# A trace of matrix products: TensorE's last products in a loop of one turn, and one block of the last long piece moved from TensorE to VectorE

## The chip, the cores and the metric

The kernel runs on one core of one Trainium2 chip. The core has TensorE (matrix products, PE in the profile; its weight loads are PEld), VectorE (DVE), ScalarE (ACT), GpSimd (POOL) and SyncE (SP), and 16 DMA engines that bring data from the chip's memory. The metric is device time in microseconds (us) of one execution, from its start to its end; lower is better. A profiled execution also has a span: from its first to its last recorded instruction.

## The reference

For each of 8 pairs of 2176 x 2176 matrices in float32 the trace of the product is wanted:

```python
def setup_inputs():
    B, N = 8, 2176
    return {
        "a": np.random.randn(B, N, N).astype(np.float32),
        "b": np.random.randn(B, N, N).astype(np.float32),
    }

def reference(a, b):
    prod = np.matmul(a, b)
    traces = np.diagonal(prod, axis1=1, axis2=2).sum(axis=-1)
    return traces.astype(np.float32)
```

The trace of a product needs no product: it is the sum over all i and k of a[i, k] * b[k, i]. So each matrix is read once, one of the two is transposed, and the rest is an elementwise product with a sum. The two inputs hold 303 MB.

## The kernel before

**Layout.** 2176 is 17 x 128. A matrix is split into three groups of rows: two of 6 x 128 and one of 5 x 128. The tiles `a_six` and `five` hold rows of a in bfloat16 (the DMA converts on the way), `rows_b` holds rows of b (and shares its first five planes with `five`), and `at` holds the transposed a, cut to fit b's rows: 17 planes of 2176 columns each, in the same places as b's.

**The main loop, once for each of 8 batches.** GpSimd issues the loads of a and b (L182). TensorE transposes a in 128 x 128 blocks into three slots of PSUM (`aT`, L242 and L245), in a hardware loop of eight turns written as `nc.Fori` over TensorE alone (L226). `hint_back_edge=True` puts a prefetch hint at the head of the loop body; the loop ends with an addition to its register and a compare-and-branch. ScalarE (L276) and VectorE (L302) copy the slots to `at`. VectorE then multiplies `at` by b's rows and sums along the row (L291), one number for each partition into `sums`.

**The last batch.** Here b arrives in ten pieces (`pieces`), the later ones smaller, so that little work is left when the last byte is down. Planes 0 to 15 come in seven pieces (`whole`). The last plane, 16 (`END`), comes in three: columns 6*128 to 2176 (eleven blocks of 128, 352 KB in the list of DMA issues), columns 2*128 to 6*128 (four blocks, 128 KB) and columns 0 to 2*128 (two blocks, 64 KB). GpSimd issues all of them about 50 us ahead of the end; each counts on a semaphore of its own (`d_late`). Behind the issues GpSimd steps a semaphore that nobody reads 20 times (`unread`, L219).

The work on them is shared:

- VectorE does the first 13 blocks of each whole plane (`SHARE` columns) and of the eleven-block piece the first ones (`N - CLOSE * P` is where its part ends; with `CLOSE = 6` that is five blocks, 640 columns), in the loop `for k, piece in enumerate(pieces[:len(whole) + 1])`.
- TensorE does the rest as matrix products of `at` and `rows_b` blocks that add up in one PSUM tile, `trace_ps`: the wanted sum is on the diagonal of that tile. For the 16 whole planes this is a second hinted loop (L252 to L256), four blocks in a turn, each turn waiting for `landed`. For the three pieces of the last plane the products are written out one by one (L262): the last six blocks of the eleven-block piece, then four, then two, each group waiting for its own piece. The last product counts on `added`.

VectorE waits for `added`, multiplies `trace_ps` by the identity and sums it (also L291, `diagonal<-identity,trace_ps`). TensorE adds up the partitions of `sums` with a product by ones (L332), after a wait for all of VectorE's parts (`parts`). VectorE reduces that to eight numbers (L334), and SyncE stores them (L339). A barrier of all engines ends the program.

**Order.** Every engine runs its instructions in the order in which they are written here; waits are on semaphores. In the program TensorE's stream is: the big loop, one product that clears `trace_ps` (L250), the loop at L252, the twelve products of L262, the sum at L332, and the closing barrier.

Of the kernel before, what the change touches and what calls it, by code (L numbers as in the profile page):

```python
# [22 lines left out]
def kernel(  # L23
# [6 lines left out]
    nc = tc.nc  # L30
    P = 128
    BATCH, N, N2 = a.shape
    assert N == N2 and N % P == 0
    NT = N // P
# [6 lines left out]
    f32 = mybir.dt.float32  # L41
    MUL, ADD = mybir.AluOpType.mult, mybir.AluOpType.add
    SLOTS = 3
    ON_TENSOR, TAKEN, CLOSE = 4, 4, 6
    SHARE = N - ON_TENSOR * P

    const = ctx.enter_context(tc.tile_pool(name="const", bufs=1))
# [15 lines left out]
    trace_ps = psum.tile([P, P], f32, tag="trace")  # L63
# [47 lines left out]
    def flat(t):  # L111
        return t.rearrange("p r k -> p (r k)")
# [10 lines left out]
    class Piece:  # L123
# [9 lines left out]
    END = NT - 1  # L133
    pieces = [
        Piece(0, 5), Piece(5, 9), Piece(9, 11), Piece(11, 13), Piece(13, 14), Piece(14, 15),
        Piece(15, 16), Piece(END, NT, 6 * P, N), Piece(END, NT, 2 * P, 6 * P), Piece(END, NT, 0, 2 * P),
    ]
# [6 lines left out]
    with tc.tile_critical(no_gpsimd_drain=True):  # L144
        def counted(name):
            return Counted(nc, name)
# [4 lines left out]
        d_late = [counted(f"late{n}") for n in range(len(pieces))]  # L151
# [6 lines left out]
        product, added = counted("product"), counted("added")  # L158
# [64 lines left out]
        pe = nc.tensor  # L223
        pe.wait_ge(ready.sem, 3)
        alone = OrderedEngineSet([pe.engine])
        with nc.Fori(0, BATCH, engines=alone, hint_back_edge=True):  # L226
            for n, (moves, _, _) in enumerate(tiles):
                use, k = divmod(n, SLOTS)
# [22 lines left out]
        x, y = flat(at), flat(rows_b)  # L251
        with nc.Fori(SHARE, SHARE + END * N, N, engines=alone, hint_back_edge=True) as first:  # L252
            pe.wait_ge(landed, 1).then_inc(landed, -1)  # L253
            for c in range(ON_TENSOR):
                block = bass.ds(first + c * P, P)
                pe.matmul(trace_ps, x[:, block], y[:, block], start=False, stop=False)  # L256
        for k, piece in enumerate(pieces):
            if piece.v1 == NT:
                pe.wait_ge(d_late[k].sem, 16)
                for c in range(N - CLOSE * P if piece.hi == N else piece.lo, piece.hi, P):  # L260
                    block = slice(END * N + c, END * N + c + P)
                    ins = pe.matmul(  # L262
                        trace_ps, x[:, block], y[:, block],
                        start=False, stop=piece.lo == 0 and c + P == piece.hi,
                    )
        added.by(ins)


        act = nc.scalar
        for n in range(BATCH):  # L270
            for t in on_scalar:
# [4 lines left out]
                ins = act.copy(out=dst, in_=view(slots[t % SLOTS]))  # L276
# [19 lines left out]
        for n in range(BATCH):  # L296
            for t in on_vector:
# [4 lines left out]
                ins = dve.tensor_copy(out=dst, in_=view(slots[t % SLOTS]))  # L302
# [14 lines left out]
        for k, piece in enumerate(pieces[:len(whole) + 1]):  # L317
# [8 lines left out]
            x, y = (t[:, piece.v0:piece.v1, piece.lo:N - CLOSE * P if close else SHARE] for t in (at, rows_b))  # L326
# [50 lines left out]
```

## Time and profile before

| | us |
|---|---|
| median of three runs | 707.95 (707.53 to 708.2) |
| the profiled execution, its own time | 707.8 |
| span of that execution | 705.8 |
| busy in the span: PE / PEld | 207.5 / 184.1 |
| busy in the span: DVE / ACT / POOL | 382.5 / 205.9 / 25.5 |

The granted TensorE clock had a mean of 0.643 over the span and was 0.50 from 670 us to the end.

How to read the lines shown below. The page begins with the span; its row "DMA" gives the mean busy share of the 16 DMA engines in 40 equal slices of the span, in tenths (9 is 90% or more), and rows that begin with q give a DMA queue, its packets, megabytes and share of the 16 engines' time. The chain of waits is followed back from the last instruction; each row has the start in us, the length in us and what the time was spent on. A timeline row has the start, the length, the engine, the source line, the operation, the tiles written and read, their shapes and a count of merged instructions; in square brackets stand the idle time of the engine before it and what ended it. A row of DMA issues ends with the size and the time from issue to landing. A row by source line gives the shortest, median and longest duration in ns, then the first and the last start in us; PEldq and POOLq are the instructions of an engine's queue that are not counted as its work, such as branches, register moves and semaphore steps.

### The profile page before, as it was taken

The page shows a single profiled execution, that of the slowest core. Times are in us where ns is not written, and L with a number is a line of the kernel's source. Part 1 is how long each engine was busy: PE and PEld are TensorE (multiplying, and loading weights), DVE is VectorE, ACT ScalarE, POOL GpSimd, SP SyncE. Part 2 cuts the span into 40 slices and gives each one's busy share as a digit, 9 for nine tenths or more (in the row PEclk, how much of TensorE's full clock was granted, in tenths as well). Part 3 has the DMA queues.
Part 4 walks back from the last instruction along what each step waited for, and adds up shares of the span by engine and source line. Part 5 has one row for each costly group of instructions (what it writes and reads, how often), then busy time and mean ns, then how long its engine had stood idle before and what let it go on. Part 6 is the DMA issues. An engine that isn't in the chain of part 4 may idle for free.

```text
span 705.8 us, 3821 instructions
## 1 busy us (share of the span) xinstructions
PE 207.5 (29%) x1575; PEld 184.1 (26%) x1575; DVE 382.5 (54%) x101; ACT 205.9 (29%) x162; POOL 25.5 (4%) x47
## 2 busy tenths in 40 slices
PE   0335013440134401244013430124301353015633
PEld 0334012440124401243013430124301242014522
DVE  0105487153971539716396163961639617395388
ACT  1427003470034600336004450044500454005800
POOL 1000000000000000000000000000000000001100
PEclk9859555685556955569556785567855677555955
DMA  9999999999999999999999999999999999999998
GB/s 235 215 216 207 231 207 213 217 225 213 223 218 213 206 214 228 213 213 229 209 211 230 214 210 223 219 213 209 231 207 213 229 213 213 224 218 213 214 212 160
DMA packets 7846, 152.12 MB, mean 216 GB/s; under 512 B 674, under 2 KB 930, under 8 KB 1442
## 3 DMA queue, kind: packets, MB, share of 16 engines
q0 software_dynamic: 7696, 150.96, 99.8%
q10 hardware_dynamic: 144, 1.11, 0.5%
q8 instruction: 1, 0.02, 0.0%
q14 instruction: 3, 0.02, 0.0%
q1 hardware_dynamic: 2, 0.00, 0.0%
HBM read 303.04 MB, written 0.00 MB: 429 GB/s over the span
## 4 chain that ended last, share of the span: by engine, by line
DMA 34%; another core or an unknown queue 28%; DVE 15%; ACT 13%; PE 7%; issue 2%; POOL 1%; SPq 0%; DVEq 0%; POOLq 0%
DMA rows_b<-in_a_dram 21%; DVE at L291 15%; ACT at L276 13%; DMA rows_b<-in_b_dram 7%; DMA a_six<-in_a_dram 6%; PE aT L242 6%; PE aT L245 1%; POOL rows_b L182 1%; PE trace_ps L262 0%; DVE diagonal L291 0%; PE total L332 0%; DVE result L334 0%; DVE sums L291 0%; DVEq L308 0%
## 5 line engine op out<-in xcount | busy, mean ns | idle before, releaser
L276 ACT COPY at<-aT 128x1536 bf16<-128x1536 bf16 (+3 forms) x160 | 202.6, 1359 | 458.2 <-DVE sums L291 357.2
L291 DVE CUSTOM_DVE_ANT_0 at<-at,rows_b 128x10880 bf16<-128x10880 bf16 (+3 forms) x18 | 278.3, 15469 | 98.5 <-DMA rows_b<-in_b_dram 83.7
L302 DVE COPY at<-aT 128x1536 bf16<-128x1536 bf16 (+1 forms) x48 | 80.1, 1669 | 207.6 <-PE aT L242 156.1
L242 PE MATMUL aT<-identity,rows_b 128*128 128x128 f32 x240 | 55.4, 422 | 368.4 <-PEq L235 282.3
L242 PEld LDWEIGHTS aT<-identity,rows_b 128*128 128x128 f32 x240 | 47.1, 220 | 374.8 <-issue 283.2
L242 PE MATMUL aT<-identity,a_six 128*128 128x128 f32 x576 | 90.5, 320 | 93.7 <-SPq L173 80.5
L242 PEld LDWEIGHTS aT<-identity,a_six 128*128 128x128 f32 x576 | 83.3, 205 | 100.3 <-issue 89.4
L245 PE MATMUL aT<-identity,a_six 128*128 128x128 bf16 x480 | 34.3, 221 | 10.8 <-ACT at L276 9.5
L245 PEld LDWEIGHTS aT<-identity,a_six 128*128 128x128 bf16 x480 | 29.4, 119 | 15.2 <-ACT at L276 13.1
L291 DVE CUSTOM_DVE_ANT_1 at<-at,rows_b 128x3328 bf16<-128x3328 bf16 (+2 forms) x4 | 23.0, 5790 | 6.1 <-DMA rows_b<-in_b_dram 6.1
L182 POOL DMA_DIRECT2D rows_b<-in_b_dram x24 | 14.2, 613 | 330.0 <-PE aT L245 330.0
L245 PE MATMUL aT<-identity,rows_b 128*128 128x128 bf16 x200 | 17.7, 266 | 0.0
L245 PEld LDWEIGHTS aT<-identity,rows_b 128*128 128x128 bf16 x200 | 17.3, 135 | 0.5
L256 PE MATMUL trace_ps<-rows_b,at 128*128 x64 | 11.3, 285 | 20.6 <-PEq L253 20.6
L182 POOL DMA_DIRECT2D rows_b<-in_a_dram x8 | 4.6, 576 | 293.6 <-DVE sums L291 292.8
L256 PEld LDWEIGHTS trace_ps<-rows_b,at 128*128 x64 | 6.7, 104 | 25.2 <-issue 23.5
L182 POOL DMA_DIRECT2D a_six<-in_a_dram x9 | 6.1, 674 | 0.0
L284 DVE MEMSET ones<- 128x1 f32 x1 | 0.1, 59 | 8.1 <-ACT rows_b L142 8.1
L142 ACT CAST rows_b<-rows_b 128x2176 bf16<-128x2176 f32 x1 | 2.0, 2004 | 3.4 <-DMA rows_b<-in_a_dram 3.4
L262 PE MATMUL trace_ps<-rows_b,at 128*128 128x128 bf16 x12 | 1.5, 310 | 0.7 <-DMA rows_b<-in_b_dram 0.7
L142 ACT ACT_TABLE_LOAD x1 | 1.3, 1283 | 1.1 <-PEq L361 1.1
L291 DVE DVE_READ_ACCUMULATOR2_ANT sums<- 128x1 f32 x17 | 1.4, 83 | 0.0
(17 smaller groups left out, 4.3 us busy)
## 6 DMA issues: line engine op xcount, KB each, us to landing
a_six<-in_a_dram POOLq DMA_DIRECT2D x7, 6528.0 KB, 54.5
rows_b<-in_b_dram POOLq DMA_DIRECT2D x7, 6528.0 KB, 52.2
rows_b<-in_b_dram POOLq DMA_DIRECT2D x8, 2720.0 KB, 21.9
rows_b<-in_a_dram POOLq DMA_DIRECT2D x7, 2720.0 KB, 24.7
a_six<-in_a_dram POOLq DMA_DIRECT2D x2, 3264.0 KB, 47.0
rows_b<-in_a_dram POOLq DMA_DIRECT2D x1, 2176.0 KB, 14.8
rows_b<-in_b_dram POOLq DMA_DIRECT2D x1, 2176.0 KB, 31.0
rows_b<-in_b_dram POOLq DMA_DIRECT2D x2, 1088.0 KB, 38.0
```

The costliest lines, as they stand in the source:

```text
L142: nc.scalar.copy(out=five[:, 0, :], in_=words)
L182: count.by(gp.dma_start(out=dst, in_=src), 16)
L242: last = pe.transpose(ps[:, place, :], src, identity32)
L245: last = pe.transpose(ps16[:, place * P:(place + 1) * P], src, identity16)
L256: pe.matmul(trace_ps, x[:, block], y[:, block], start=False, stop=False)
L262: ins = pe.matmul(trace_ps, x[:, block], y[:, block], start=False, stop=piece.lo == 0 and c + P == piece.hi,)
L276: ins = act.copy(out=dst, in_=view(slots[t % SLOTS]))
L284: ready.by(dve.memset(ones, 1.0))
L291: return dve.tensor_tensor_reduce(out=x if out is None else out, in0=x, in1=y, scale=1.0, scalar=0.0, op0=MUL, op1=ADD, accum_out=acc,)
L302: ins = dve.tensor_copy(out=dst, in_=view(slots[t % SLOTS]))
```

## The change

The products of L262 are put into a hardware loop of one turn, on TensorE alone, with the same kind of hint as the two loops before it. Its count comes from a register that is set to 1 just ahead. `CLOSE` goes from 6 to 5: of the eleven-block piece TensorE now does the last five blocks (eleven products in all) and VectorE the first six (768 columns).

```diff
-    ON_TENSOR, TAKEN, CLOSE = 4, 4, 6
+    ON_TENSOR, TAKEN, CLOSE = 4, 4, 5
...
-        for k, piece in enumerate(pieces):
-            if piece.v1 == NT:
-                pe.wait_ge(d_late[k].sem, 16)
-                for c in range(N - CLOSE * P if piece.hi == N else piece.lo, piece.hi, P):
-                    block = slice(END * N + c, END * N + c + P)
-                    ins = pe.matmul(
-                        trace_ps, x[:, block], y[:, block],
-                        start=False, stop=piece.lo == 0 and c + P == piece.hi,
-                    )
-        added.by(ins)
+        once = nc.alloc_register(pe.engine, "once")
+        pe.reg_mov(once, 1)
+        with nc.Fori(0, pe.snap(once, min_val=1, max_val=BATCH), engines=alone, hint_back_edge=True):
+            for k, piece in enumerate(pieces):
+                if piece.v1 == NT:
+                    pe.wait_ge(d_late[k].sem, 16)
+                    for c in range(N - CLOSE * P if piece.hi == N else piece.lo, piece.hi, P):
+                        block = slice(END * N + c, END * N + c + P)
+                        ins = pe.matmul(
+                            trace_ps, x[:, block], y[:, block],
+                            start=False, stop=piece.lo == 0 and c + P == piece.hi,
+                        )
+            added.by(ins)
```

On TensorE's queue the built program gains, between the loop at L252 and the sum, three register moves and a prefetch hint ahead of the products, and an addition and a compare-and-branch behind them; a matrix product (with its weight load) is gone. The wait for each piece stays with that piece's first product. No other engine's instructions change but for VectorE's one longer product. Line numbers behind L256 are three higher after the change: L262 becomes L265, L332 becomes L335.

## The prediction

> **What bounds the kernel now.** I read the page first, then the chain of waits, then the timeline of the last microseconds, where all of the change lies.
>
> ```profile
> span 705.8 us, 3821 instructions
> ...
> DMA  9999999999999999999999999999999999999998
> ...
> q0 software_dynamic: 7696, 150.96, 99.8%
> ```
>
> The DMA engines are full in 39 of 40 slices, so up to the last byte no engine's work sets the time. What a change at the very end can move is the stretch behind that byte. The chain in order of time shows it:
>
> ```profile
> 650.02 3.64 POOL rows_b L182 x7
> 653.66 47.79 DMA rows_b<-in_b_dram
> 701.45 0.05 issue
> 701.50 1.48 PE trace_ps L262 x12
> 702.97 0.02 issue
> 703.00 0.29 DVE diagonal L291
> 703.28 0.02 DVE sums L291
> 703.30 0.04 issue
> 703.35 0.28 PE total L332 x2
> 703.63 0.02 issue
> 703.65 0.18 DVE result L334
> ```
>
> The transfer that starts at 653.66 lands at 701.45. TensorE's twelve written-out products (L262) follow, then VectorE's read of the diagonal, the sum on TensorE (L332) and VectorE's last reduction. The chain hides that inside the 1.48 us of L262 two more transfers land. The answers on the last DMA issues, and narrow stretches of the timeline, show them:
>
> ```profile
> 654.18 1.14 POOL L182 DMA_DIRECT2D rows_b<-in_b_dram  x2
> rows_b<-in_b_dram POOLq DMA_DIRECT2D x1, 128.0 KB, 47.9
> rows_b<-in_b_dram POOLq DMA_DIRECT2D x1, 64.0 KB, 47.7
> L262 PE MATMUL trace_ps<-rows_b,at x12: 289/314/314, 701.5 to 702.6; 128*128 128x128 bf16 x12
> 701.68 0.63 PE L262 MATMUL trace_ps<-rows_b,at 128*128 128x128 bf16 x4
> 702.13 0.61 PE L262 MATMUL trace_ps<-rows_b,at 128*128 128x128 bf16 x4
> 702.46 0.23 PEld L262 LDWEIGHTS trace_ps<-rows_b,at 128*128 128x128 bf16 x2
> ```
>
> The first row holds the last two issues. The four-block piece is issued at 654.18 and lands 47.9 later, at 702.08; the two-block piece is issued at about 654.70 and lands at 702.4. Four matmuls take 0.63 us and one 0.314, so one block follows another in (0.63 - 0.314) / 3 = 0.105 us. The first block of the four-block piece starts at 702.13, 0.05 us behind its landing, and the weights behind the last wait are loaded at 702.46, about 0.05 us behind theirs. The first piece started 0.05 us behind its landing too (701.45, 701.50). All three starts are set by landings.
>
> **One block from TensorE to VectorE.** The six blocks of the long piece, at 0.105 us each from 701.50, would let the next block start at 702.13, exactly where the landing lets it start. With five blocks TensorE is ready at 702.03 and waits for the same landing. So a whole block, 0.105 us, is removed and at most that is gained; I take nothing, because the start at 702.13 has the same 0.05 us behind its landing as the other two. From 702.13 the remaining six blocks run as before, to 702.97.
>
> VectorE's closing product grows from 640 to 768 columns:
>
> ```profile
> 699.74 1.89 DVE L291 CUSTOM_DVE_ANT_0 at<-at,rows_b 128x1664 bf16<-128x1664 bf16 x1 [0.15 <-DMA rows_b<-in_b_dram]
> ...
> 701.56 0.82 DVE L291 CUSTOM_DVE_ANT_0 at<-at,rows_b 128x640 bf16<-128x640 bf16 x1
> ...
> 703.00 0.29 DVE L291 CUSTOM_DVE_ANT_0 diagonal<-identity,trace_ps 128x128 bf16<-128x128 f32 x1 [0.61 <-PE trace_ps L262]
> ...
> 703.86 0.32 SPq L339 DMA_DIRECT2D out_dram<-result  x1
> ```
>
> 1,024 columns more cost 1.89 - 0.82 = 1.07 us, so 128 cost 0.13. VectorE had 0.61 us idle before the diagonal, which it needs at 703.00; 0.48 remain. Cost nothing; without that cover 0.13.
>
> **Entering the loop.** Between the old loop's exit and the first product TensorE's queue gets three register moves and a prefetch hint (and a branch that, like the one ahead of the loop at L252, should leave no row of its own). The same kinds, at L252:
>
> ```profile
> L252 PEldq MOVE  x2: 29/34/38, 668.6 to 668.8; - x2
> L252 PEldq BRANCH_PREFETCH_HINT  x1: 31/31/31, 668.7 to 668.7; - x1
> L252 PEldq ALU_OP  x1: 36/36/36, 700.5 to 700.5; - x1
> L252 PEldq COMPARE_BRANCH  x1: 80/80/80, 700.6 to 700.6; - x1
> ```
>
> Move, hint and move stand 0.1 us apart. The old loop's last branch ends at 700.6 + 0.08 = 700.7; four instructions at 0.1 bring TensorE to 701.1, and it waits for 701.45 anyway. Cover 0.35 us; cost nothing, and without the cover 0.4, of which the block taken away would give back 0.1.
>
> **Leaving the loop.** An addition and a compare-and-branch now stand between the last product and the sum L332 (L335 after). When can they run? The exit of the big loop at L226 tells:
>
> ```profile
> 666.55 0.53 PE L245 MATMUL aT<-identity,a_six 128*128 128x128 bf16 x6 [0.48 <-ACT at L276]
> L226 PEldq ALU_OP  x1: 36/36/36, 666.6 to 666.6; - x1
> L226 PEldq COMPARE_BRANCH  x1: 80/80/80, 666.7 to 666.7; - x1
> L249 PEldq EVENT_SEMAPHORE  x1: 51/51/51, 666.8 to 666.8; - x1
> ```
>
> Its addition runs as the last wait is released (666.55), before the six matmuls behind that wait end (667.08); the branch falls through in 0.08 us, and the next instruction is there 0.1 us on, although the loop was hinted to go back. In the new loop the last wait is released at 702.46, so the branch is done by about 702.7. The sum waits for VectorE until 703.30. Cover 0.6 us; cost nothing, provided that the code behind the loop is at hand.
>
> **The code behind the loop** is the open price. One 16 KB instruction transfer runs in the last microseconds of the trace, the only one on its queue:
>
> ```profile
> q0 software_dynamic: 222, 0.13, 90.7%
> q8 instruction: 1, 0.02, 6.1%
> ```
>
> That is the window from 701 to 702; a window from 701.6 to 701.8 has it starting there.
>
> ```profile
> q8 instruction: 1, 0.02, 30.6%
> ```
>
> 30.6% of 16 engines over 0.2 us is 0.98 us of one engine, so it is done at about 702.7. I take it for TensorE's: it starts about 1.1 us behind the exit of TensorE's loop, and no other engine leaves a loop. Then TensorE asks for code at or after 700.6 and has it 2.1 us later, with the twelve products already in its queue and covering the load. [...] If the missing code begins right behind the loop, the request falls at about 702.6 and the sum waits until 702.6 + 2.1 = 704.7 in place of 703.35: +1.4 us. The other bound is the slowest such load of the trace: GpSimd's run of 20 semaphore steps ends at 655.7, and a small instruction transfer follows only at 659.2.
>
> ```profile
> L219 POOLq EVENT_SEMAPHORE  x20: 17/17/17, 653.8 to 655.7; - x20
> q14 instruction: 1, 0.01, 20.1%
> ```
>
> The second row is the window 659.2 to 659.3. That is 3.5 us to the start under full DMA; with 0.98 for 16 KB it is 4.5, and the sum would come at 707.1, +3.8 us. At the other end the missing code is that of the closing barrier, which TensorE needs only at 704 and later: nothing. I take nothing for the forecast, because the added code is about six instructions and the boundary must fall in a narrow place to hurt; both ends stay in the range.
>
> [...]
>
> **Sum.** Block 0, VectorE 0, entry 0, exit 0, code 0: the profiled 707.8 us (a span of 705.8 and 2.0 around it) stays. It lies 0.15 below the median of 707.95; I forecast 708.0.
>
> **Rivals.**
> 1. Exposed code load. One mechanism: the code behind the one-turn loop is asked for only at 702.6, and the sum L335 stands behind it. For it: a code transfer does happen in the tail, and the change puts a stop in the queue between it and its cover. Against: the exit at L226 needed none. It gives 708 + 1.4 = 709.4, at most 711.8; it decides from the moment when the load takes more than 703.30 - 702.6 = 0.7 us.
> 2. Faster, because the code transfer leaves the last data microseconds. The packet starts at 701.77; the four-block piece lands at 702.08, so at most 0.3 us earlier, 707.6. Against: two of three pieces were down or almost down when it began. More than this no row offers.
> 3. The loop starts TensorE late: entry longer than its 0.35 us of cover. With twice the 0.4 counted, 0.45 late, less one block: +0.35, 708.3.
> 4. The change does not do what it says: the hint changes no code transfer, which stays at 701.8. Then 707.95.
>
> **How the numbers follow.** 0.2% of 708 is 1.4 us, about what a measurement of this kernel can tell from no change. Forecast with rival 4: 0.48, 707.6 to 708.3. Rival 1: 0.38, of which about 0.27 falls above 709.4, since its nearest row lies just at that bound and its far end well above. Rivals 2 and 3: 0.07 each; 0.05 of rival 2 stands for a gain beyond 1.4 us that I see in no row, and 0.03 of rival 3 for such a loss. So faster 0.05, slower 0.27 + 0.03 = 0.30, same 0.65. The range goes from 707.3 to 710.1: it leaves out the upper half of rival 1's far part and a larger gain.
>
> **What would show it.** Right: the first product 0.05 us behind the first landing, a short wait between the fifth product and the four-block piece, and the sum about 0.9 us behind the last landing, as now (702.4 to 703.35). Rival 1: a 16 KB instruction transfer after 702.5 and an idle TensorE before L335 while VectorE's last part is long done. Rival 2: no transfer, and shorter times from issue to landing. Rival 3: the first product more than 0.1 us behind its landing. A span that differs before 700 us would make the whole reading wrong, since nothing there is changed.

## The result and the profile after

The changed kernel is slower: a median of 710.63 us over 18 runs (708.01 to 711.07) against 707.44 us of 18 runs of the kernel before (707.13 to 708.2). The measured ratio is 1.0037, with a 95% interval of 1.0031 to 1.0044; it is smaller than that of the two medians (1.0045), and three of the 18 runs of the changed kernel are hardly slower (708.0 to 708.4). The profiled execution took 710.91 us. The page of the changed kernel, its first line, the DMA slices and the DMA queues:

```profile
span 705.6 us, 3825 instructions
...
DMA  9999999999999999999999999999999999999998
...
q0 software_dynamic: 7696, 150.96, 99.8%
q10 hardware_dynamic: 144, 1.11, 0.5%
q14 instruction: 3, 0.02, 0.0%
q1 hardware_dynamic: 2, 0.00, 0.0%
```

The span did not grow. It is 0.2 us shorter than before (705.6 against 705.8), and DMA is as full. The loss lies outside the span: before, the execution lasted 2.0 us longer than its span (707.8 - 705.8), now 5.3 us (710.9 - 705.6). And one row of the queues is gone: the 16 KB instruction transfer on q8, which the kernel before made in the window from 701.6 to 701.8. The chain of waits of the changed kernel, in order of time (start, length, what):

```profile
653.41 47.80 DMA rows_b<-in_b_dram
701.21 0.05 issue
701.26 1.46 PE trace_ps L265 x11
702.72 0.02 issue
702.74 0.29 DVE diagonal L294
703.03 0.02 DVE sums L294
703.05 0.04 issue
703.09 0.28 PE total L335 x2
703.37 0.02 issue
703.39 0.18 DVE result L337
```

From the landing at 701.21 to the last reduction it takes 2.18 us; before it took 2.20 (701.45 to 703.65). Inside the span the change did nothing, as the sum had it. The list of TensorE's own instructions by line, and the timeline of its weight loads, show why:

```profile
L259 PEldq MOVE  x2: 29/32/35, 700.6 to 700.7; - x2
L259 PEldq BRANCH_PREFETCH_HINT  x1: 31/31/31, 700.8 to 700.8; - x1
L259 PEldq ALU_OP  x1: 36/36/36, 702.2 to 702.2; - x1
L259 PEldq COMPARE_BRANCH  x1: 86/86/86, 702.3 to 702.3; - x1
...
701.25 0.45 PEld L265 LDWEIGHTS trace_ps<-rows_b,at 128*128 128x128 bf16 x5 [0.91 <-DMA rows_b<-in_b_dram]
701.88 0.56 PEld L265 LDWEIGHTS trace_ps<-rows_b,at 128*128 128x128 bf16 x6 [0.17 <-DMA rows_b<-in_b_dram]
```

The hint is done at 700.8, ahead of the landing at 701.21; the first five products start 0.05 us behind it, wait 0.17 us for the four-block piece, and the loop's branch is done at 702.4, 0.7 us ahead of the sum. Then a window of the DMA engines from 707.4 to 708.7, beyond the span, has what is missing:

```profile
DMA packets 1, 0.02 MB, mean 13 GB/s; under 512 B 0, under 2 KB 0, under 8 KB 0
...
q8 instruction: 1, 0.02, 5.8%
```

All of it is counted in the first of the window's 40 slices, 504 GB/s over 0.0325 us, which is 16 KB; 5.8% of 16 engines over 1.3 us is 1.2 us of one engine. The transfer comes 5.6 us later than before (707.4 against 701.8), alone, with every recorded instruction of the program already done. No row names the code that a transfer brings. I take it for the one that the kernel before made at 701.8, since each of the two executions has just one. The closing barrier does not wait for it: TensorE's rows of that barrier, before and after, are complete inside the span, about 0.3 us earlier than before, as the landing is.

```profile
L372 PEldq EVENT_SEMAPHORE  x3: 51/51/51, 5.8 to 705.8; - x3
L372 PEldq DRAIN  x2: 8/8/8, 704.4 to 705.5; - x2
...
L375 PEldq EVENT_SEMAPHORE  x3: 51/51/51, 5.9 to 705.5; - x3
L375 PEldq DRAIN  x2: 8/8/8, 704.1 to 705.2; - x2
```

So what waits for it, if anything does, has no row. The experiments were made to find out whether it is the loop, the hint or the moved block that put it there, and whether it is this load that the 3.3 us go to.

### The profile page after: what moved, and what is told of

Read it like the earlier page. It is cut to its first block, busy times and chain, and to the rows that moved or that the text cites. A ratio compares the mean times of both kernels' runs of the same rounds, so it can differ in the third digit from the quotient of the medians.

```text
span 705.6 us, 3825 instructions
## 1 busy us (share of the span) xinstructions
PE 205.9 (29%) x1574; PEld 182.4 (26%) x1574; DVE 382.7 (54%) x101; ACT 205.8 (29%) x162; POOL 25.5 (4%) x47
## 4 chain that ended last, share of the span: by engine, by line
DMA 34%; another core or an unknown queue 28%; DVE 15%; ACT 14%; PE 6%; issue 2%; POOL 1%; SPq 0%; DVEq 0%; POOLq 0%
DMA rows_b<-in_a_dram 21%; DVE at L294 15%; ACT at L279 14%; DMA rows_b<-in_b_dram 7%; DMA a_six<-in_a_dram 6%; PE aT L242 5%; PE aT L245 1%; POOL rows_b L182 1%; PE trace_ps L265 0%; DVE diagonal L294 0%; PE total L335 0%; DVE result L337 0%; DVE sums L294 0%; DVEq L311 0%
## 5 line engine op out<-in xcount | busy, mean ns | idle before, releaser
L256 PE MATMUL trace_ps<-rows_b,at 128*128 x64 | 11.3, 285 | 20.7 <-PEq L253 20.7
L256 PEld LDWEIGHTS trace_ps<-rows_b,at 128*128 x64 | 6.7, 104 | 25.3 <-issue 23.5
L265 PE MATMUL trace_ps<-rows_b,at 128*128 128x128 bf16 x11 | 1.4, 309 | 0.7 <-DMA rows_b<-in_b_dram 0.7
```

Source lines behind the costliest of these rows:

```text
L265: ins = pe.matmul(trace_ps, x[:, block], y[:, block], start=False, stop=piece.lo == 0 and c + P == piece.hi,)
```

## The experiments

For each kernel below, "behind" is a run's time less its span, that is, the time outside the recorded instructions. Over 100 runs of the kernel before that ran beside the experiments, behind was at most 2.0 us in every one. 63 of them had a span of 705.3 to 705.7 (short) and 37 one of 705.9 to 706.3 (long); what separates these two is found below.

**The parts alone.** e1 is the kernel before with the block moved and no loop, e2 the changed kernel with the block moved back, e3 the changed kernel without the hint:

```diff
e1, to the kernel before
-    ON_TENSOR, TAKEN, CLOSE = 4, 4, 6
+    ON_TENSOR, TAKEN, CLOSE = 4, 4, 5
e2, to the changed kernel
-    ON_TENSOR, TAKEN, CLOSE = 4, 4, 5
+    ON_TENSOR, TAKEN, CLOSE = 4, 4, 6
e3, to the changed kernel
-        with nc.Fori(0, pe.snap(once, min_val=1, max_val=BATCH), engines=alone, hint_back_edge=True):
+        with nc.Fori(0, pe.snap(once, min_val=1, max_val=BATCH), engines=alone):
```

> The kernel before with CLOSE = 5 alone, no third loop. If the loop is the whole cause: 707.4, ratio 0.999 to 1.001, the 16 KB instruction transfer inside the last data microseconds (about 701.5), the closing part behind the span about 2 us as before. If the moved block is the cause: about 710.6.

> The hinted loop of one turn alone, CLOSE = 6. If the loop is the cause: about 710.6, ratio 1.003 to 1.005, a span of about 705.5 and 5 us behind it, with the 16 KB instruction transfer only behind the span, near 707.4. If the moved block is the cause: 707.4.

> The changed kernel with its one-turn loop kept and its hint left out. Theory A, the hint keeps TensorE from reading the next code block ahead: 707.4, the transfer back near 701.5, span about 0.3 us longer than the changed kernel's. Rival B, any loop's branch does it: 710.6 and the transfer behind the span.

| | median (range), 10 runs | ratio (95%) | behind over 2.5 us |
|---|---|---|---|
| e1, block moved | 707.35 (707.12 to 708.07) | 0.9998 (0.9989 to 1.0008) | 0 of 10 |
| e2, hinted loop | 709.12 (707.22 to 710.65) | 1.0023 (1.0011 to 1.0036) | 6 of 10 |
| e3, loop without hint | 707.34 (707.19 to 708.12) | 1.000 (0.9991 to 1.001) | 0 of 10 |
| changed kernel | 710.63 (708.01 to 711.07), 18 runs | 1.0037 (1.0031 to 1.0044) | 15 of 18 |

The moved block alone is nothing. The loop without its hint is nothing. The hint is the cause. Among the runs with a short span, behind is over 2.5 us in 15 of 15 of the changed kernel and 6 of 7 of e2, and in none of 7 of e1 and none of 7 of e3. Leaving out the hint also shifts the code behind it by one instruction; but e2, whose code is one product longer than the changed kernel's, loses time as well, so the shift does not explain it. e2's expectation was met only in part: four of ten runs escaped, and the six spread from 3.0 to 5.0 us behind, where the changed kernel has 3.7 to 5.4; whether the moved block makes the loss more frequent under the hint, ten runs do not tell.

Where the 16 KB transfer lay in the profiled executions of these kernels is read from windows of the DMA engines. e1, from 701.3 to 702.3, and e3, from 672.6 to 673.7, in this order:

```profile
q8 instruction: 1, 0.02, 5.8%
```

```profile
q8 instruction: 1, 0.02, 5.4%
```

e1 has it where the kernel before had it. e3's profiled execution has it 29 us earlier, against its expectation, and none in the tail: the place is not fixed. That execution had a span of 706.0 us. It is the first sign of the question that e7 is about.

**The load pulled into the span.** e4 adds 24 TensorE instructions behind the sum, so that TensorE comes to the missing code sooner:

```diff
+        for _ in range(12):
+            pe.matmul(slots[0][:, 0, 0:1], diagonal, diagonal[:, 0:1], start=True, stop=True)
```

> The changed kernel with twelve one-column products of zeros behind the sum of the partitions, into a PSUM slot that nobody reads any more: 24 more TensorE instructions without a hint between the loop's exit and the closing barrier. If the next block is asked for when TensorE comes within reach of its boundary, or some instructions behind the last hinted loop: the transfer moves to 702 to 705, behind the data and ahead of the end of the span, and the time falls to about 707.2, under the kernel before. If the place where it is asked for lies inside the loop and is passed for good: 710.6, the transfer still behind the span.

Measured: 708.99 (707.82 to 709.41), ratio 1.0017 (1.0007 to 1.0027). Neither branch came out as written. The time behind the span is back at 1.8 to 1.9 us in all ten runs, but six of them have a span of 707.1 to 707.5, and the other four 706.0 to 706.4. The loss has moved with the instructions, from outside the span to inside it. Only TensorE's instructions were changed, so this points to TensorE, waiting for code that starts within 24 instructions of its last recorded one; that is a conclusion from the spans. The wait itself is not seen in e4: its profiled execution is one of the four with the shorter span (706.1), and has a 16 KB instruction transfer already at 671.5.

**How much of the tail has to be under the hint.** e5 keeps only the first five products in the hinted loop, e6 only the last six:

```diff
e5, to the changed kernel; the other pieces' products stand behind the loop
-                if piece.v1 == NT:
+                if piece.v1 == NT and piece.hi == N:
e6, to the changed kernel; the first piece's products stand ahead of the loop
-                if piece.v1 == NT:
+                if piece.v1 == NT and piece.hi < N:
```

> The changed kernel with only the first piece's five products in the hinted loop of one turn; the other six are written out behind it, so TensorE stands outside a hinted loop from 701.5 instead of 702.4, with twelve more instructions ahead of the sum. If TensorE reads ahead whenever it works on outside a hinted loop for about a microsecond, or while it passes the last six products: 707.3, transfer near 702. If one more hint in the tail is enough to put it off: 710.6, transfer behind the span.

> The changed kernel with the first piece's five products written out and only the last six in the hinted loop. Between the loop at L252 and the new hint lie ten products' instructions, issued at once, and about 1 us of waiting for the first piece. If the read-ahead is set off by passing a place among the first five products, or needs about a microsecond without a hint: 707.3, transfer near 701.5. If it is set off among the last six products or by the sum: 710.6.

Measured: e5 708.07 (707.94 to 710.78), ratio 1.0013 (1.0003 to 1.0022); e6 708.9 (707.23 to 710.77), ratio 1.0022 (1.0013 to 1.0032). Seven of e5's runs had a span of 705.9 to 706.2 and lay at most 2.1 us behind it; the three with a short span lay 3.7, 4.3 and 5.1 behind. e5's profiled execution, one of these three, has its only 16 KB instruction transfer at 706.8, behind its span of 705.6, as the changed kernel has. In both, the execution's own time ends 2.2 to 2.3 us after the end of that transfer (2.3 us after 708.6, 2.2 after 707.8, if time and span are counted from the same start). Of e6's ten runs, seven lay 2.6 to 5.4 behind; its profiled execution is one of the other three, with the transfer at 702.0. So neither place in the tail decides, and in e5 six products behind the hinted loop did not spare the three runs that lay 3.7 to 5.1 behind. Both branches of both expectations were too simple: with a hint in either place some runs lose time behind the span, by an amount that differs from run to run.

**The load made visible.** e9 and e10 put a loop of two turns, with one harmless product in it, ahead of the sum of the changed kernel; in e10 that loop has a hint too:

```diff
e9, to the changed kernel
+        twice = nc.alloc_register(pe.engine, "twice")
+        pe.reg_mov(twice, 2)
...
+        with nc.Fori(0, pe.snap(twice, min_val=1, max_val=BATCH), engines=alone):
+            pe.matmul(slots[0][:, 0, 0:1], diagonal, diagonal[:, 0:1], start=True, stop=True)
```

> The changed kernel with a loop of two turns without a hint between the one-turn loop and the sum, its body a one-column product of zeros into a slot that nobody reads. Theory C, the read-ahead is set off when TensorE leaves a loop whose branch has jumped back at least once, which a loop of one turn never does: the transfer comes at about 704, 2 us behind the span as in the kernel before, 707.5 to 707.8 (the loop itself delays the sum by 0.2 to 0.4). Theory D, the hint of the one-turn loop alone puts the read-ahead off for several microseconds, whatever follows: 710.6 to 711.

> As e9, the loop of two turns hinted like the kernel's other loops. Theory C: as e9 by its jump, 707.6 to 707.9. Theory D: one more hint, 710.6 to 711.

Measured: e9 708.73 (708.21 to 709.05), ratio 1.0014 (1.0005 to 1.0024), with 1.7 to 1.8 us behind the span in all ten runs; e10 711.17 (710.51 to 711.99, four runs), ratio 1.0051 (1.0036 to 1.0066). For e9 neither theory's time came out: the loop cost more than I had written (the sum starts 0.9 us later than it could), and no load is exposed behind the span. For e10 about theory D's time came out, but in another place: the loss is inside the span, which grew to 708.1 to 710.2 in the four runs and 709.0 in the profiled one. Its TensorE instructions by line and its timeline show it, then the window of the DMA engines from 703.1 to 704.2:

```profile
L337 PEldq MOVE  x2: 29/32/35, 702.9 to 703.0; - x2
L337 PEldq BRANCH_PREFETCH_HINT  x2: 31/34/36, 705.6 to 706.2; - x2
...
702.76 0.08 DVE L296 DVE_READ_ACCUMULATOR2_ANT sums<- 128x1 f32 x1
705.73 0.11 PEld L338 LDWEIGHTS aT<-diagonal 128*128 128x128 bf16 x1 [3.49 <-issue]
705.74 0.18 PE L338 MATMUL aT<-diagonal 128*128 128x1 bf16 x1 [3.23 <-issue]
706.24 0.10 PEld L338 LDWEIGHTS aT<-diagonal 128*128 128x128 bf16 x1 [0.40 <-issue]
706.25 0.18 PE L338 MATMUL aT<-diagonal 128*128 128x1 bf16 x1 [0.32 <-issue]
...
706.79 0.18 DVE L341 TENSOR_REDUCE result<-total 1x8 f32<-1x32 f32 x1 [3.95 <-PE total L339]
```

```profile
q8 instruction: 1, 0.02, 5.2%
```

TensorE's second register move runs at 703.0, and the next instruction of its stream, the hint, at 705.6. It waits for no semaphore in between (the idle time is put down to "issue"), VectorE has long been done, and VectorE's last reduction sits idle for 3.95 us. In that gap, from about 703.2, lies the 16 KB transfer, 0.9 us of one engine (5.2% of 16 engines over 1.1 us). This is the exposed load in the open: 2.6 us from the last instruction at hand to the next, of which the transfer is 0.9. The other 1.5 us lie behind the transfer. The 3.3 us that the changed kernel loses behind its span are of the same size; that they are a wait of the same kind is concluded from e4 and e10, not seen, since nothing behind the closing barrier leaves a row. e10's wait is at any rate at another place: ahead of the sum, where the changed kernel has its code. And a late transfer is no loss by itself: e10 has a second one at 710.0 and e2's profiled execution a second one at 707.4, both behind the span, and these executions lie only 1.8 and 2.0 us behind.

**The two spans.** e7 takes the hint from the second loop of the kernel before, e8 puts the product ahead of that loop under a hint, e11 moves that product to the start:

```diff
e7, to the kernel before
-        with nc.Fori(SHARE, SHARE + END * N, N, engines=alone, hint_back_edge=True) as first:
+        with nc.Fori(SHARE, SHARE + END * N, N, engines=alone) as first:
e8, to the kernel before; the lines with + replace the same three lines without a loop
+        once = nc.alloc_register(pe.engine, "once")
+        pe.reg_mov(once, 1)
+        with nc.Fori(0, pe.snap(once, min_val=1, max_val=BATCH), engines=alone, hint_back_edge=True):
+            pe.wait_ge(scalar_done.sem, BATCH)
+            pe.wait_ge(vector_done.sem, BATCH)
+            pe.matmul(trace_ps, diagonal, diagonal, start=True, stop=False)
e11, to the kernel before; SyncE takes the product's two waits ahead of the pieces, and the product leaves its old place
         pe.wait_ge(ready.sem, 3)
+        pe.wait_ge(zeros.sem, 3)
+        pe.matmul(trace_ps, diagonal, diagonal, start=True, stop=False)
```

> The kernel before with the hint of its second loop (L252) left out, so that TensorE is without a hint from 666.7 on. Theory: the read-ahead comes at 670 to 673 in every run, under full DMA, and the engine that carries it stays late to the end: span 706.1 and time 708.0 in every run, where the kernel before has both 707.3 and 708.0. Rival, that late engine has another cause: the mix stays as before.

> The kernel before with the two waits and the product ahead of its second loop (L250) in a hinted loop of one turn, so that only about 0.4 us in place of 1.9 us lie without a hint between the big loop and the second. Theory: no transfer at 670 to 673 or fewer of them, nearly all runs 707.1 to 707.5, mean 0.1 to 0.2 us under the kernel before, the transfer near 701.5. Rival, the mix does not depend on it: as the kernel before.

> The kernel before with the product that clears trace_ps (L250) moved ahead of the big loop and its two waits moved to SyncE ahead of the pieces, so that the second loop's hint follows the big loop's exit by about 0.3 us in place of 2. A version meant to beat both: if the read-ahead at 670 needs the 2 us without a hint, every run is at 707.1 to 707.4, mean about 0.2 us under the kernel before. If not, the mix of 707.3 and 708.0 stays, as with e8.

e7: 707.96 (707.81 to 708.04), ratio 1.0006 (0.9996 to 1.0015); all ten runs have a span of 706.0 to 706.3, as expected. Two windows of the DMA engines of its profiled execution, from 675.4 to 676.4 and from 702.1 to 702.8, when e1 moves no data any more:

```profile
q8 instruction: 1, 0.02, 5.8%
...
q0 software_dynamic: 11, 0.01, 5.5%
```

The load comes at 675.4, in the middle of the data and a few microseconds later than expected. At the end 5.5% of 16 engines are busy, that is 0.9 of one engine: as much as one DMA engine that still moves its share when the others are done (which engines move it, the window does not tell), and the last data packet ends at 702.6, where e1's ends at 701.8. The profiled executions of all kernels fall into the same groups:

| profiled execution | 16 KB instruction transfers, start | last data packet ends | span | behind |
|---|---|---|---|---|
| the kernel before | 701.8 | 702.1 | 705.8 | 2.0 |
| e1, e6, e11, e12 | 701.3 to 702.0 | 701.7 to 701.8 | 705.3 to 705.5 | 1.8 to 1.9 |
| e3, e7, e8 | 672.7 to 675.4 | 702.4 to 702.6 | 706.0 to 706.3 | 1.7 to 2.0 |
| e2, e4 | 670.2 and 707.4; 671.5 and 704.1 | 702.5 | 706.1 to 706.2 | 1.9 to 2.0 |
| the changed kernel, e5 | 707.4; 706.8 | 701.9 | 705.6 | 5.3; 4.3 |
| e9 | 672.7 | 702.4 | 707.0 | 1.7 |
| e10 | 703.2 and 710.0 | 701.7 | 709.0 | 1.8 |

Wherever a load came at 670 to 676, under full DMA, the data end 0.6 to 0.9 us later than in e1, e6, e11 and e12, and the span is 0.5 to 1.0 us longer (e9 apart, whose added loop lengthens it too). One in the tail or behind the data costs the data nothing: they end at 701.8 with it in e1 and at 701.9 without it in the changed kernel. The profiled execution of the kernel before, with its load in the tail, lies between the groups; its transfers were also issued 0.2 us later than the changed kernel's (650.02 against 649.78). That the late DMA engine is the one that carried the code is likely and not shown, since no row names the engine. The 37 of 100 runs of the kernel before with a long span took 707.67 to 708.13, e7's runs 707.81 to 708.04; in the changed kernel the same three spans (706.1 to 706.3) belong to the only three runs that lie no more than 2.1 us behind it. By their spans, these had their code in time. A long span is no proof of that, though: in e6, three of the seven runs that lie 2.6 us or more behind (2.6 to 2.9) have a span of 706.1 or 706.2, and no trace shows why.

e8: 707.28 (707.18 to 708.07), ratio 1.000 (0.9991 to 1.0009), with 5 of 11 runs at the long span against 12 of 33 beside it: no fewer, so the expectation failed. e11: 707.33 (707.21 to 707.93), ratio 0.9996 (0.9987 to 1.0005), 2 of 11 against 12 of 21 beside it: fewer, but not none, as the theory had it. It was run again:

> The kernel of e11 once more, since 2 of its 11 runs against 12 of 21 of the kernel before had the late engine (a span of 705.8 or more), too few to tell. If the shorter time without a hint matters: again at most 2 or 3 of about 11, and a mean 0.1 to 0.25 us under the kernel before. If that was chance: the same share as the kernel before in this call, a third to a half, and the same mean.

Measured: 707.38 (707.18 to 708.01), ratio 1.000 (0.9991 to 1.0009), 2 of 11 against 3 of 15, and the same mean, 707.46. No version that beats the kernel before was found.

## Why the prediction was right or wrong

The likeliest case, 708.0 us and no change, did not come; what came is, by the conclusion from e4 and e10, an exposed code load as in rival 1, which had 0.38, at a place that I had not given it. The median is 0.5 us above the top of the range, although the forecast started 0.5 us too high: three runs of the kernel before gave 707.95, 18 gave 707.44. The change itself is +3.2 us, where next to nothing was forecast.

- **One block to VectorE, taken as 0: right.** e1 is at 0.9998, and the wait of 0.17 us between the two groups of weight loads shows that landings pace TensorE. VectorE's longer product was covered by the 0.48 us forecast (the diagonal waits 0.47 in the changed kernel and 0.48 in e1).
- **Entering and leaving the loop, taken as 0: right.** The hint is done 0.4 us ahead of the landing and the last branch 0.7 us ahead of the sum; the whole loop without its hint (e3) costs nothing.
- **"I take nothing for the forecast, because the added code is about six instructions and the boundary must fall in a narrow place to hurt": this step failed.** It looked at the six instructions as something that shifts a boundary, and passed over what the hint itself does. With the hint of the one-turn loop 15 of 18 runs lie over 2.5 us behind the span, without it none of ten (e3); in the profiled executions the 16 KB transfer starts at 707.4 with that hint and at 672.7 without it, and for the hint of the second loop at 701.8 with it and at 675.4 without it (e7). The code was not missing for the sum, which starts 0.04 us after VectorE's last part, and not for the recorded rows of the closing barrier, but, as far as e4 and e10 allow the conclusion, for what TensorE has to run behind them. The prediction's harmless end of its bounds, the closing barrier, "which TensorE needs only at 704 and later: nothing", took for granted that a load asked for in the tail would be there by then; it came at 707.4. The price was in the bounds: 3.3 us behind the span, and 2.6 us where it can be seen (e10), against the +1.4 to +3.8 of rival 1. That the upper bound is so near is luck: no run shows that the small transfer at 659.2, from which it was worked out, was one that GpSimd waited for.
- **"I take it for TensorE's": right**, by e10, where TensorE's next instruction stands behind it, and by e4. The +1.4 us of rival 1 was not: it was worked out from a request for code at about 702.6, at the exit of the loop, and no run shows one there. In the changed kernel the loop's branch is done at 702.4 and the transfer starts 5.0 us later, at 707.4; e3 has the same addition and branch and no loss (a ratio of 1.000).
- **Rival 2, data landing earlier without the transfer: wrong.** The four-block and the two-block piece take 47.9 and 47.7 us to land, before and after.
- **Rival 3, the loop starts TensorE late: wrong.** The first product starts 0.05 us behind its landing, as before.
- **Rival 4, the transfer stays at 701.8: wrong** with the hint (707.4). Without it the time is that of no change (e3, 707.34), but e3's profiled execution has the transfer at 672.7.

The row that spoke for the right answer was there: the one instruction transfer of the tail, 1.1 us behind the exit of a hinted loop. It was used for a price and not for the question of what sets it off, which the edit touches directly.

All 100 runs of the kernel before, and all of e1 and e3, lie at most 2.0 us behind their spans. With a hinted loop in the tail 2.6 us were lost inside e10's span and about 3.3 us behind the changed kernel's. In the changed kernel it is not a jump that costs them: the one-turn loop's branch does not jump back (0.09 us, against 0.23 us for the one of e9 that does).

**What stays open** is what exactly decides when the 16 KB instruction transfer comes. Two edits show that a hint matters: without the hint of its second loop the kernel before has a long span in ten of ten runs (e7, whose profiled execution has the transfer at 675.4) and with it in 37 of 100; without the hint of the one-turn loop the time behind the span is over 2.5 us in none of ten runs (e3) and with it in 15 of 18. In the profiled execution of the kernel before the transfer comes about a microsecond after leaving the second loop (700.7, 701.8). e5, e6 and e8 speak against one place in the code, or the length of the stretch without a hint, as what alone decides. Theory C of e9 (a loop that has jumped back sets the reading of code off) is not refuted, but e9 cannot confirm it: its profiled execution had the transfer already at 672.7, and for the other nine the spans, 706.4 to 707.3, do not tell whether it came early or during the added loop. Open is also what, if anything, TensorE runs behind the closing barrier.

## What to carry to other kernels

An edit that only touches control flow can cost time where no instruction is recorded: compare the execution's own time with its span, and look at the instruction transfers outside the span, before saying that a tail is unchanged. In this kernel a hint for a loop's jump back was not free in the tail: on the loop that never jumps back it cost 0.13% (e5) to 0.37% (the changed kernel), and the same loop without it cost nothing (e3). Before pricing such an edit, find the instruction transfer that it may move, and name everything that needs that code, what lies behind the program's last recorded instruction included.

## What the runs showed of the hardware

A 16 KB instruction transfer took 0.9 to 1.3 us of one DMA engine in the profiled executions, by its share of their windows (0.9 in e1, e7 and e10, 1.2 in the changed kernel, 1.3 in e4), but 2.6 us passed from TensorE's last instruction at hand to its next (e10, 703.0 to 705.6), with no other transfer in that time. A transfer of the same size in the middle of full DMA (e7, at 675.4) goes with data that end 27 us after it and 0.8 us later than in e1 (702.6 against 701.8), and with a span about 0.7 us longer (706.2 in place of 705.5). So the cheapest moment for it here is the tail, as in most runs of the kernel before by their spans (63 of 100), where it overlaps the last products and costs neither: in e1 it starts at 701.3, the data end at 701.8, and the execution lies 1.9 us behind a span of 705.5. With the hint of the one-turn loop the transfer came at 707.4 in the changed kernel's profiled execution, behind the program's last recorded instruction, and 15 of 18 runs lay over 2.5 us behind the span; without that hint (e3) it came at 672.7, and none of ten runs did.
